# The order of the VectorE and ScalarE queues of a hybrid decoder trunk taken from the framework's timeline simulation

## The chip, the cores and the metric

The kernel runs on one core of a Trainium2 chip. The metric is the device time of one execution in microseconds (us). The kernel before took 970.87 us, the median of three runs (970.82 to 971.13).

A core has engines that work side by side, each through a queue of its own, strictly in order: TensorE (PE: matrix products; its weight loads are listed apart as PEld), VectorE (DVE: element-wise work, reductions), ScalarE (ACT: functions and scaled copies), GpSimd (POOL) and SyncE (SP), which here issues most DMAs. An instruction whose operands are not ready holds up everything behind it in the same queue, whether or not that could have started. This is what an order of a queue can cost, and it is the only thing that this change touches.

## The reference

Sixteen learned rows are set ahead of 512 tokens (L = 528 rows of 1024). Two layers follow, each a pre-normed branch that is added to its input, and a final norm; the sixteen rows are dropped.

```python
h = concat([meta, x])                                  # 528 x 1024
# layer 1: gated linear attention, 4 heads of 256 (k) x 512 (v)
q, k, v, z, g_lr = split(rmsnorm(h, g_norm[0]) @ gla_w_in)
lg = log_sigmoid(g_lr @ w_gate_up + b_gate) / 16       # decay, low rank
o  = chunked_scan(q, k, v, lg)                         # state S decayed per chunk
h  = h + (silu(z) * head_rms(o) * gla_gnorm) @ gla_w_out
# layer 2: differential softmax attention, 8 heads, two softmaxes each
q, k, v, z = split(rmsnorm(h, g_norm[1]) @ diff_w_in)
lam = exp(sum(lv[0]*lv[1])) - exp(sum(lv[2]*lv[3])) + lambda_init
a  = softmax(q0 k0 + bias) - lam * softmax(q1 k1 + bias)
h  = h + (silu(z) * head_rms(a @ v) * diff_gnorm * (1 - lambda_init)) @ diff_w_out
out = rmsnorm(h[16:], g_final)
```

## The kernel before

Everything is float32. A matrix product is made of rounded parts: `split` (L270 to L280) writes the high part of a tile with a ScalarE copy (L276) and the rest with a VectorE subtraction (L277), and TensorE adds high times high, high times low and low times high. So every weight block and every operand passes through ScalarE first and VectorE second before TensorE can use it. In the profile these are `wh` and `wl` (a pair of weight blocks), `a11h`, `a12h`, `a22h` and their `l` halves (single blocks), and `x`, `y`, `aT` (operands). `split3` (L402 to L411) does the same for narrow tiles `am`, `vm` and `cm` (ScalarE on L407 and L408, VectorE on L410 or L412).

The large input projections run as units of seven products in place of eight (class `Unit`). A product (`product`, L428, matmuls on L431) fills a PSUM bank `bx`, `by` or `bv`; there are two `bx` banks and one each of the others. When the first product of a unit ends, ScalarE copies it out as `u` (`partial`, L452), and only then can the bank be filled again; VectorE adds later products to that copy (L477 to L481). Sums of weight blocks are VectorE additions (L366). The first projections go without this scheme (`plain_unit`, L878).

The program starts by loading tokens, norming and turning them, and splitting them in pairs of tiles `x` (L776 scales a tile `y`, L277 makes the low parts). TensorE then computes the narrow projection of the decay (L1001, `bx<-x,kd`) from these tiles while the first value projection (L878) fills its gaps. Beside this, three short operations on VectorE read tiny tensors whose loads SP issues one after the other on L666, L668 and L671: `gn_sb` is halved (L1071), `dgs` is made from `dg_sb` (L1105), and `lt` is the product of the lambda vectors `lv` (L1097). They are first wanted a long time later: `lt` by a matmul near 143 us, `gn_sb` near 95 us. L796, L800 and L801 are differences and sums of halves of `y` for the units.

In layer 2 a head's work on one block of rows is: scores (matmuls on L400), VectorE adds the bias and finds the minimum (L1692), ScalarE takes the exponential (L1694), VectorE combines the two softmaxes (`st` on L1697 and L1698, the probabilities `p` on L1699), TensorE transposes `p` (L1707 and L1708) and multiplies by the values. The output projection of the head before runs between these (L400 with `bx`, `by`, `bv` as targets), and VectorE adds it to `keep` (L1783).

What sets the order. TensorE's order is written out by hand: `manual_schedule` for PE covers all of `trunk`, and a `Weaver` puts pieces of the projections between pieces of attention by estimated times. For VectorE and ScalarE the order is fixed by hand only at the start (L720 to L1031, for the instructions issued between these lines) and, on VectorE, for the last rows. Everywhere else the framework orders these two queues, and SP's, from dependencies, priorities and its estimate of when things are ready. The kernel steers it with priorities (`urgent`, `soon`, `at_once`, L254 to L265) and a few forced successions (`issue_after`). An instruction whose inputs the framework takes to be ready, and which appears much later in the program, can thus be moved ahead, as the three short operations are.

```python
    def urgent(fn, offset=100):

        def run(*a, **kw):
            with tc.high_priority(offset=offset):
                return fn(*a, **kw)
        return run
...
        @at_once
        def partial(self):
            t = T(up[0], [P, HT], F32, "u", bufs=3)[:, :self.n]
            W.moved = act.activation(t, self.bx[:, :self.n], AF.Copy, scale=self.sc)
            return t
```

Of the kernel before, what the change touches and what calls it, by code (L numbers as in the profile page):

```python
# [1944 lines left out]
def build(shapes):  # L1945
    import concourse.bacc as bacc

    nc = bacc.Bacc("TRN2", target_bir_lowering=False, num_devices=1, dynamic_dma_scratch_size=512)
    args = [nc.dram_tensor(f"in_{n}_dram", shp, F32, kind="ExternalInput").ap() for n, shp in shapes]
    args.append(nc.dram_tensor("out_0_dram", (1, NR, D), F32, kind="ExternalOutput").ap())  # L1950
    with tile.TileContext(nc) as tc:
        trunk(tc, *args)
    return nc

# [14 lines left out]
```

## Time and profile before

| what | value |
|---|---|
| median of 3 runs | 970.87 us |
| the profiled execution itself | 970.65 us |
| its span, first to last instruction | 968.9 us |
| outside the span | 1.75 us |
| TensorE busy | 957.2 us (99%) |
| VectorE busy | 778.6 us (80%) |
| ScalarE busy | 626.8 us (65%) |
| GpSimd busy | 44.9 us (5%) |
| mean granted TensorE clock | 0.999 |

A row of the timeline gives start, duration, engine, line, operation, output and inputs, a count where like neighbours are joined, and in brackets how long the engine idled before it and what ended that. A row of the windows gives a stretch, then for each engine its busy time and the number of its instructions, then the granted TensorE clock (1.00 is full), the share of the DMA engines and GB/s. A row of the waits gives who waited for whom: total, times, longest.

### The profile page before, as it was taken

How to read it: one execution, taken by the hardware profiler on the slowest of the kernel's cores; microseconds unless marked ns; L12 is line 12 of the kernel's file. 1: busy time of each engine (PE TensorE's matmuls, PEld its weight loads, DVE VectorE, ACT ScalarE, POOL GpSimd, SP SyncE). 2: the span in 40 equal slices, each digit the busy share in tenths (PEclk: the TensorE clock that was granted, in tenths of full speed). 3: DMA queues.
4: the chain of work that ended last, by engine and by line, in shares of the span. 5: the costliest groups of instructions: out<-in, count | busy, mean ns of one | idle time of the engine just before them, and what ended most of it. 6: DMA issues, size and time to landing. Idle time of an engine off the chain costs nothing.

```text
span 968.9 us, 18048 instructions
## 1 busy us (share of the span) xinstructions
PE 957.2 (99%) x6993; PEld 906.9 (94%) x6993; DVE 778.6 (80%) x1586; ACT 626.8 (65%) x1304; POOL 44.9 (5%) x68
## 2 busy tenths in 40 slices
PE   9999999999999999999999999999999999999997
PEld 8999999999999999998899998998999989989996
DVE  7989885886888787668997987968869769687785
ACT  7776755577647567656757776575675756755583
POOL 1000000000000000000001001000000000000001
PEclk9999999999999999999999999999999999999999
DMA  7322223635363236124355525243342341722212
GB/s 197 88 85 59 82 79 122 147 103 128 116 162 91 85 117 158 53 101 152 99 130 138 143 73 133 75 139 98 99 138 88 118 119 44 182 70 84 89 64 87
DMA packets 128522, 104.94 MB, mean 108 GB/s; under 512 B 51102, under 2 KB 112830, under 8 KB 128433
## 3 DMA queue, kind: packets, MB, share of 16 engines
q1 hardware_dynamic: 123104, 93.80, 35.1%
q10 hardware_dynamic: 5328, 9.95, 2.8%
q8 instruction: 56, 0.92, 0.4%
q14 instruction: 34, 0.27, 0.1%
HBM read 83.64 MB, written 11.80 MB: 99 GB/s over the span
## 4 chain that ended last, share of the span: by engine, by line
PE 88%; ACT 1%; DVE 1%; issue 1%; POOLq 0%; DVEq 0%
PE bx L431 19%; PE bv L431 12%; PE by L431 10%; PE bx L421 10%; PE ps L400 9%; PE bx L972 5%; PE bx L400 3%; PE bv L972 2%; PE by L972 2%; PE ps L1214 2%; PE by L400 2%; PE bv L400 2%; PE ps L1807 1%; PE bx L1807 1%; PE bv L421 1%; PE by L421 1%
## 5 line engine op out<-in xcount | busy, mean ns | idle before, releaser
L277 DVE TENSOR_TENSOR wl<-raw,wh 128x1024 fp32r<-128x1024 f32 x98 | 119.4, 1221 | 23.0 <-ACT wh L276 18.9
L276 ACT ACTIVATE wh<-raw 128x1024 fp32r<-128x1024 f32 x98 | 103.1, 1054 | 48.3 <-PE by L972 22.9
L431 PE MATMUL bv<-x,wh 128*128 128x264 f32 (+1 forms) x656 | 98.6, 287 | 0.0
L431 PE MATMUL bx<-x,wh 128*128 128x264 f32 (+1 forms) x640 | 95.6, 286 | 0.0
L431 PEld LDWEIGHTS bv<-x,wh 128*128 128x128 f32 x656 | 86.8, 189 | 0.6 <-DVE z L479 0.2
L431 PEld LDWEIGHTS bx<-x,wh 128*128 128x128 f32 x640 | 84.6, 188 | 0.7 <-ACT u L452 0.2
L452 ACT ACTIVATE u<-bx 128x264 f32<-128x264 f32 (+1 forms) x120 | 45.3, 379 | 35.5 <-PE bx L431 33.1
L1694 ACT ACTIVATE p<-p,st 128x528 f32<-128x528 f32 (+3 forms) x64 | 36.5, 570 | 41.7 <-DVE st L1692 41.4
L421 PE MATMUL bx<-x,wh 128*128 128x512 f32 (+1 forms) x256 | 62.4, 385 | 0.0
L277 DVE TENSOR_TENSOR wl<-sum,wh 128x1024 fp32r<-128x1024 f32 x41 | 50.1, 1221 | 10.6 <-ACT wh L276 10.5
L431 PE MATMUL bx<-x,wl 128*128 128x264 f32 (+1 forms) x320 | 54.1, 284 | 0.0
L431 PE MATMUL bv<-x,wl 128*128 128x264 f32 (+1 forms) x328 | 53.8, 284 | 0.1
L421 PEld LDWEIGHTS bx<-x,wh 128*128 128x128 f32 x256 | 44.4, 188 | 7.8
L276 ACT ACTIVATE wh<-sum 128x1024 fp32r<-128x1024 f32 x41 | 43.1, 1051 | 9.7 <-PE by L972 3.9
L431 PE MATMUL by<-x,a12h 128*128 128x264 f32 (+1 forms) x320 | 47.5, 286 | 0.1
L1730 POOL TENSOR_TENSOR st<-st,mhalf 128x1 f32<-128x1 f32 x32 | 25.5, 795 | 468.6 <-ACT on L1728 418.2
L431 PE MATMUL bx<-x,a11h 128*128 128x264 f32 (+1 forms) x320 | 46.6, 284 | 0.0
L431 PEld LDWEIGHTS bv<-x,wl 128*128 128x128 f32 x328 | 45.4, 188 | 0.3 <-issue 0.3
L431 PEld LDWEIGHTS bx<-x,wl 128*128 128x128 f32 x320 | 45.3, 188 | 0.3
L431 PEld LDWEIGHTS bx<-x,a11h 128*128 128x128 f32 x320 | 42.4, 188 | 0.6
L431 PEld LDWEIGHTS by<-x,a12h 128*128 128x128 f32 x320 | 42.1, 188 | 0.3 <-ACT t L1658 0.3
L276 ACT ACTIVATE a11h<-raw 128x512 fp32r<-128x512 f32 x41 | 25.7, 626 | 20.7 <-DMA raw<-in_diff_w_in_dram 7.9
(493 smaller groups left out, 2631.9 us busy)
## 6 DMA issues: line engine op xcount, KB each, us to landing
raw<-in_gla_w_in_dram SPq DMA_DIRECT2D x48, 512.0 KB, 4.5
raw<-in_diff_w_in_dram SPq DMA_DIRECT2D x42, 512.0 KB, 4.9
raw<-in_diff_w_in_dram SPq DMA_DIRECT2D x11, 1024.0 KB, 5.9
raw<-in_gla_w_out_dram SPq DMA_DIRECT2D x8, 1024.0 KB, 5.8
raw<-in_diff_w_out_dram SPq DMA_DIRECT2D x8, 1024.0 KB, 6.0
vd<-planes ACTq DMA_DIRECT2D x12, 268.0 KB, 5.8
vd<-keep ACTq DMA_DIRECT2D x12, 264.0 KB, 2.3
T<-bdr SPq DMA_DIRECT2D x8, 264.0 KB, 4.7
```

Source lines behind the costliest of these rows:

```text
L276: act.activation(hi, src, AF.Copy)
L277: dve.tensor_tensor(lo, src, hi.bitcast(F32), op=ALU.subtract)
L400: pe.matmul(ps, l, r, start=first and n == 0, stop=last and n == 2, **kw)
L421: pe.matmul(bank, a[:, k, :], b[k] if n0 is None else b[k][:, n0 + i * nn:n0 + (i + 1) * nn], start=n == 0 and ks[0] == 0, stop=n == len(t ...
L431: pe.matmul(bank[:, :x[q].shape[2]], w[p][:, k * P:(k + 1) * P], x[q][:, k, :], start=first and i == 0, stop=i == len(PASSES) - 1, skip_gr ...
L452: W.moved = act.activation(t, self.bx[:, :self.n], AF.Copy, scale=self.sc)
L972: pe.matmul(banks[i][:, :HT], h.t[p][:, k, mm * P:(mm + 1) * P], s.y[q][k][:, i * HT:(i + 1) * HT], start=n == 0, stop=n == len(PASSES) - 1)
L1214: pe.matmul(o, s.kd[:, i, kc], s.qs[:, i, t0:t0 + n], start=i == 0, stop=i == 1)
L1694: act.activation(p[:, :nk], p[:, :nk], AF.Exp, scale=-1.0, bias=st[:, m:m + 1], accum_out=st[:, 2 + m:3 + m])
L1730: pool.tensor_tensor(ms, ms, mhalf[:, :1], op=ALU.pow)
L1807: pe.matmul(ps[i], yp[hd][p][:, k, b * P:(b + 1) * P], wt[q][cs.start // 512][:, 2 * hd + k, cs.start % 512:(cs.stop - 1) % 512 + 1], star ...
```

## The change

One argument is added where `build` opens the framework's context. With it, the framework orders the queues that are not ordered by hand by a simulated timeline of the program in place of its plain estimate of readiness.

```diff
-    with tile.TileContext(nc) as tc:
+    with tile.TileContext(nc, schedule_with_timeline_sim=True) as tc:
         trunk(tc, *args)
```

No instruction is added or taken away, and none changes its shape. TensorE's and GpSimd's queues stay as they were. VectorE's and ScalarE's are reordered over the whole program (1810 and 1172 lines of difference), and on SP some DMAs change places with a neighbour (43 lines). Three places follow; a minus marks where a row stood, a plus where it stands now.

VectorE at the start of the program (about 17 to 25 us), where the tiles `x` are split in pairs:

```order
 L776 TENSOR_SCALAR y_42_291<-ps_276,g_sb 128x512
+L1071 TENSOR_SCALAR gn_sb<-gn_sb 128x16
+L1105 TENSOR_SCALAR dgs<-dg_sb 128x2
+L1097 TENSOR_TENSOR lt_4700<-lv 128x2
 L277 TENSOR_TENSOR x_1_77<-y_35_258,x_1_77 128x528
 L277 TENSOR_TENSOR x_34_257<-y_35_258,x_34_257 128x528
 L274 TENSOR_TENSOR wl_269<-raw_131,wh_268 128x1024
 L776 TENSOR_SCALAR y_42_291<-ps_286,g_sb 128x512
+L796 TENSOR_TENSOR y_35_258<-y_35_258 128x4x264
 L277 TENSOR_TENSOR x_2_78<-y_42_291,x_2_78 128x528
 L277 TENSOR_TENSOR x_3_79<-y_42_291,x_3_79 128x528
```

The three operations on the tiny loads moved up by some twenty rows to a place ahead of the second `x` pair, and L796 moved ahead of the third and fourth.

ScalarE at about 189 to 192 us, in a unit of layer 1; `u_5261` is the copy that frees a `bx` bank, `v` and `vm` are operands of the value products, `a11h` a weight block of the next unit:

```order
 L276 ACTIVATE wh_5225<-raw_4940 128x1024
-L575 ACTIVATE v_885_4661<-keep_83,tick_5242 128x4x128
+L575 ACTIVATE v_885_4661<-keep_83,tick_5242 128x4x128 x2
+L407 ACTIVATE vm_884_4660<-lands_5085,short 32x256
+L276 ACTIVATE a11h_5253<-raw_5081 128x512
+L408 ACTIVATE vm_884_4660<-lands_5085,short 32x256
 L452 ACTIVATE u_5261<-bx_5238 128x264
-L276 ACTIVATE a11h_5253<-raw_5081 128x512
-L575 ACTIVATE v_885_4661<-keep_83,tick_5242 128x4x128
 L276 ACTIVATE a12h_5315<-raw_5081 128x512
-L407 ACTIVATE vm_884_4660<-lands_5085,short 32x256
-L408 ACTIVATE vm_884_4660<-lands_5085,short 32x256
```

The copy `u_5261` now stands behind four instructions that stood behind it.

VectorE at about 862 to 870 us, in a head of layer 2; `p_13569` are the probabilities that TensorE transposes next. Before:

```order
L277 TENSOR_TENSOR wl_13605<-raw_13530,wh_13604 128x1024
L1699 SCALAR_TENSOR_TENSOR p_13569<-p_13581,st_13568,p_13569 128x528
L1692 ISA p_13626,st_13625<-ps_13627,T_13186 128x400
L1692 ISA st_13625 128x1
L1692 ISA p_13633,st_13625<-ps_13634,T_13186 128x400
L1692 ISA st_13625 128x1
L1783 TENSOR_TENSOR keep_8187<-keep_8187,by_13521 128x512
L1783 TENSOR_TENSOR keep_8187<-keep_8187,bv_13522 128x512
L1697 RECIPROCAL st_13625<-st_13625 128x1
L1783 TENSOR_TENSOR keep_8187<-keep_8187,bx_13523 128x512
L1698 SCALAR_TENSOR_TENSOR st_13625<-st_13625,lam 128x1
L277 TENSOR_TENSOR wl_13673<-raw_13530,wh_13672 128x1024
```

On the same engine at the same place of the program, after the change:

```order
L277 TENSOR_TENSOR wl_13605<-raw_13530,wh_13604 128x1024
L1697 RECIPROCAL st_13568<-st_13568 128x1
L366 TENSOR_TENSOR raw_13540<-raw_13540,sum_13682 128x4x128
L1783 TENSOR_TENSOR keep_8187<-keep_8187,by_13521 128x512
L1692 ISA p_13626,st_13625<-ps_13627,T_13186 128x400
L1692 ISA st_13625 128x1
L1783 TENSOR_TENSOR keep_8187<-keep_8187,bv_13522 128x512
L1698 SCALAR_TENSOR_TENSOR st_13568<-st_13568,lam 128x1
L1783 TENSOR_TENSOR keep_8187<-keep_8187,bx_13523 128x512
L277 TENSOR_TENSOR wl_13673<-raw_13530,wh_13672 128x1024
L1699 SCALAR_TENSOR_TENSOR p_13569<-p_13581,st_13568,p_13569 128x528
```

`p_13569` (L1699) moved from directly behind `wl_13605` to behind `wl_13673`, with the addition of `bx_13523` (L1783) between.

## The prediction

> **What bounds the kernel now.** I began with the page: busy times, the chain that ended last, and the two groups that speak of the parts made by ScalarE and VectorE.
>
> ```profile
> PE 957.2 (99%) x6993; PEld 906.9 (94%) x6993; DVE 778.6 (80%) x1586; ACT 626.8 (65%) x1304; POOL 44.9 (5%) x68
> ...
> PE 88%; ACT 1%; DVE 1%; issue 1%; POOLq 0%; DVEq 0%
> ...
> L277 DVE TENSOR_TENSOR wl<-raw,wh 128x1024 fp32r<-128x1024 f32 x98 | 119.4, 1221 | 23.0 <-ACT wh L276 18.9
> ...
> L452 ACT ACTIVATE u<-bx 128x264 f32<-128x264 f32 (+1 forms) x120 | 45.3, 379 | 35.5 <-PE bx L431 33.1
> ```
>
> TensorE is busy for 957.2 of 968.9 us, so it idles for 11.7 in all. The windows say where.
>
> ```profile
> 0.00:20.00 20.00, 18.08 (x130) 16.87 (x130) 14.31 (x35) 15.17 (x28) 3.42 (x11) 1.00 0.88 238
> 20.00:60.00 40.00, 39.66 (x329) 39.00 (x327) 35.69 (x54) 32.50 (x66) 0.00 (x0) 1.00 0.33 80
> ...
> 960.00:969.00 9.00, 2.12 (x16) 1.78 (x14) 3.58 (x8) 2.35 (x7) 0.86 (x1) 0.84 0.31 117
> ```
>
> The first row has 1.9 us of idle TensorE, the last 6.9, where nothing is left to multiply; everything between has 11.7 - 1.9 - 6.9 = 2.9. The waits of TensorE name most of it:
>
> ```profile
> PE bx L421 <- DVE wl L277: 0.7, 1, 0.7
> PE ps L1244 <- DVE vm L412: 0.7, 1, 0.7
> PE ps L1214 <- DVE kd L1218: 0.5, 1, 0.5
> ```
>
> So a new order of VectorE and ScalarE can give back some 2.9 us at most in the middle, while TensorE's order, which is written by hand, stands still and waits for whatever comes late. In 20 to 60 us VectorE is busy for 35.69 of 40: there it has little room to catch up. The question is thus where an operand comes later than TensorE's use of it, and each place is worked out as: how much later the row ends, less the slack that it had.
>
> **The start: three operations on tiny loads.** The order has L1071, L1105 and L1097 ahead of the second `x` pair, and L796 ahead of the third and fourth. Where they ran before, on VectorE:
>
> ```profile
> 18.33 1.33 DVE L277 TENSOR_TENSOR x<-y,x 128x528 fp32r<-128x528 f32 x2 [0.56 <-ACT x L276]
> ...
> 21.37 1.31 DVE L277 TENSOR_TENSOR x<-y,x 128x528 fp32r<-128x528 f32 x2
> ...
> 24.98 1.25 DVE L796 TENSOR_TENSOR y<-y 128x1056 f32<-128x1056 f32 x1
> ...
> 30.04 0.17 DVE L1071 TENSOR_SCALAR gn_sb<-gn_sb 128x16 f32<-128x16 f32 x1
> 30.12 0.16 DVE L1105 TENSOR_SCALAR dgs<-dg_sb 128x2 f32<-128x2 f32 x1
> ...
> 30.77 0.16 DVE L1097 TENSOR_TENSOR lt<-lv 128x2 f32<-128x2 f32 x1
> ```
>
> They take half a microsecond, but they need loads, and the last of these was issued by SP after the second pair had ended. The other row is of a like load, with its time from issue to landing at the end:
>
> ```profile
> 20.98 0.47 SPq L671 DMA_DIRECT2D lv<-in_diff_lam_dram  x1
> ```
>
> ```profile
> short<-in_short_dram SPq DMA_DIRECT2D x1, 2.2 KB, 1.8
> ```
>
> ```profile
> 22.50:23.00 0.50, 0.50 (x6) 0.50 (x5) 0.50 (x2) 0.50 (x2) 0.00 (x0) 1.00 0.48 20
> 23.00:23.50 0.50, 0.50 (x7) 0.50 (x6) 0.50 (x1) 0.50 (x2) 0.00 (x0) 1.00 0.04 0
> ```
>
> Its packets still run until 23.0 (DMA share 0.48, then 0.04), so `lv` lands at 23.0 at the earliest. By the like load it would be 20.98 + 0.47 + 1.8 = 23.25. `lv` is gathered element by element, and landing is told after the last packet, so I take 24.0 with 23.0 and 24.5 as ends. SP's issues up to `lv` keep their order, so this time stays. VectorE therefore halts from about 18 to 24.0, and with 0.16 for `lt` the pair of 18.33 starts at 24.2, 5.9 late. The pair of 21.37 is late by that and by L796's 1.25: 7.1. TensorE uses them here:
>
> ```profile
> 20.67 0.36 PE L1001 MATMUL bx<-x,kd 128*112 128x264 f32 x1
> ...
> 23.73 0.73 PE L1001 MATMUL bx<-x,kd 128*112 128x264 f32 x4
> ```
>
> The first half of the first pair ended at 19.0 and would end at 24.9: TensorE stands still at 20.67 for some 4.2. The second pair ended at 22.68; of the four matmuls at 23.73 the third and fourth, near 24.06, are the first to read it, so the slack was 1.4 and TensorE ends up 7.1 - 1.4 = 5.7 late. I take 5.5 (4.5 with the early landing, 6.2 with the late one). The projections of L878 that could fill the hole stand behind in TensorE's own queue.
>
> **The probabilities at 866 us.** L1699 of one block moved behind `wl_13673`, which waits for ScalarE.
>
> ```profile
> 863.80 0.76 DVE L1699 SCALAR_TENSOR_TENSOR p<-p,st,p 128x528 f32<-128x528 f32 x1
> ...
> 867.88 1.23 DVE L277 TENSOR_TENSOR wl<-raw,wh 128x1024 fp32r<-128x1024 f32 x1 [0.28 <-ACT wh L276]
> ```
>
> ```profile
> 866.58 0.60 PE L1707 MATMUL ps<-ident,p 128*128 128x128 f32 x4
> ```
>
> `wl` ends at 869.1 and L1699 then at 869.1 + 0.7 = 869.8; the transposes at 866.58 wait until then: 3.2. The same move with other blocks finds its time covered.
>
> **Copies `u` that free a bank.** At nine places L452 moved behind work that another product could wait for. The place that the order shows, on ScalarE and then TensorE:
>
> ```profile
> 189.52 0.37 ACT L452 ACTIVATE u<-bx 128x264 f32<-128x264 f32 x1
> 189.79 0.62 ACT L276 ACTIVATE a11h<-raw 128x512 fp32r<-128x512 f32 x1
> 190.31 0.71 ACT L575 ACTIVATE v<-keep,tick 128x512 fp32r<-128x512 f32 x1
> ...
> 191.45 0.49 ACT L407 ACTIVATE vm<-lands,short 32x256 fp32r<-32x256 f32 x1
> 191.97 0.51 ACT L408 ACTIVATE vm<-lands,short 32x256 fp32r<-32x256 f32 x1
> ```
>
> ```profile
> 190.61 1.14 PE L431 MATMUL bx<-x,wh 128*128 128x264 f32 x8
> ```
>
> `u` ended at 189.89, 0.72 ahead of the product that refills its bank. Four instructions go ahead of it, 0.5 apart for three of them and 0.6 for L575 (starts overlap a little): about 1.9 to 2.2. That leaves 1.2 to 1.5; I take 1.2. The same exchange comes once more a head later. In layer 2 the same unit meets the same exchange in four heads; the first:
>
> ```profile
> 643.96 0.37 ACT L452 ACTIVATE u<-bx 128x264 f32<-128x264 f32 x1
> ...
> 644.47 0.39 ACT L276 ACTIVATE aT<-ps 128x256 fp32r<-128x256 f32 x1
> 644.75 0.25 ACT L407 ACTIVATE am<-ps 32x128 fp32r<-32x128 f32 x1
> 645.01 0.27 ACT L408 ACTIVATE am<-ps 32x128 fp32r<-32x128 f32 x1
> ```
>
> ```profile
> 644.54 0.53 PE L431 MATMUL bx<-x,wh 128*128 128x264 f32 x3
> ```
>
> Here the slack is 644.54 - 644.33 = 0.21, and the three rows of `aT` and `am`, and the issue of a DMA, now go first: 0.8 for the three, 1.1 with the issue, so 0.6 to 0.9, and I take 0.8. The three other places of this kind lie between, and I give them 0.9. Sum: 2 x 1.2 + 4 x 0.8 + 3 x 0.9 = 8.3.
>
> **Five more places** have an operand of TensorE behind one to three instructions that now go first: L1255 twice and L1731 behind high parts of weights, L1403 behind a `wl` (1.22 by its group), the low part of `v` (L277) behind L801 early on. Not worked out each, they get the mean of the nine, 8.3 / 9 = 0.92: 4.6 (an estimate; nothing to 1.5 each).
>
> **What goes away, and what costs nothing.** Where TensorE waited for `wl`, `vm` and `kd`, the new order has these rows further ahead: at most 0.7 + 0.7 + 0.5 and some tenths, 2.2. On SP, the load of the bias table goes ahead of weights that are split only many rows later; at a wrong moment that would be one issue, about a microsecond. All other moves on VectorE and ScalarE stay inside the time by which their results lie ahead of TensorE; were that cover gone, each would cost what its neighbour lasts, 0.4 to 1.2.
>
> **The sum.** 5.5 + 3.2 + 8.3 + 4.6 - 2.2 = 19.4. Against the profiled execution, 970.65 + 19.4 = 990.05; the median of the runs is 0.22 above that execution, so 990.3.
>
> **The clock.** The granted clock could make it more. In the last window of the first table TensorE's final 2.12 us of work are over at 962.1, and then:
>
> ```profile
> 965.00:966.00 1.00, 0.00 (x0) 0.00 (x0) 0.10 (x1) 0.07 (x1) 0.00 (x0) 1.00 0.04 14
> 966.00:967.00 1.00, 0.00 (x0) 0.00 (x0) 0.00 (x0) 0.00 (x0) 0.00 (x0) 0.56 1.00 383
> ```
>
> With 0.56 as the mean of that microsecond the clock fell to half at 966.1, after 4.0 us of idle TensorE; the stall of the start would be 4.2. What half a clock costs is seen at the start, where the same eight transposes took 1.70 and later 1.09:
>
> ```profile
> 5.66 1.70 PE L705 MATMUL ps<-ident,qs 128*128 128x128 f32 x8
> ```
>
> ```profile
> 9.01 1.09 PE L705 MATMUL ps<-ident,ks 128*128 128x128 f32 x8 [0.19 <-ACT hT L711]
> ```
>
> The slow pace there lasted from the first matmul, near 1 us, to about 7, so a fall could cost half of 6 us, 3.0, or less where the clock comes back sooner: nothing to 3, and if it falls I take 2.5. Every other stall that I count is shorter than the 4.0 us of idleness that the trace shows ahead of the fall, so this can happen once. [...]
>
> **The rivals.**
> 1. Only the long halts count. Many of the fourteen places under 1.5 us have their price from one trace, and a queue that is late at one place has been early at the one before; if ScalarE's and VectorE's idle time (968.9 - 626.8 = 342 and 968.9 - 778.6 = 190 us) takes them up, 5.5 + 3.2 - 2.2 = 6.5 is left: 977.4. For it: `u` in its group idled 33.1 us behind TensorE, so ScalarE is mostly there early. Against it: the slack in the rows, 0.21 and 0.72, has that in it already. Chance 0.15.
> 2. The clock falls in the first stall: 990.3 + 2.5 = 992.8. For it: 4.2 of stall against 4.0 of idleness ahead of the fall that the trace shows. Against it: the margin is a few tenths, and an early landing of `lv` (23.0) shortens the stall to 3.2. Chance 0.15.
> 3. The other side: VectorE reaches L1071 no earlier than its loads have landed, because what stands ahead of the pair at 18.33 comes late as well, or `lv` lands sooner than its packets let me think, and ScalarE's moves fall into idle time. Then only the waits go: 970.87 - 2.2 = 968.7. It decides at a landing of `lv` by about 19, against an issue at 20.98. Chance 0.05.
> 4. The moves cancel, a few tenths each way, within 0.2% (1.9 us, about what a measurement of this kernel can tell from no change): 970.9. It needs the halt at the start to be absent too. Chance 0.03.
> 5. More late places than I followed, or longer ones, since 1810 and 1172 lines move: ten more at 0.92 give 999.5. Chance 0.10.
>
> My forecast, all places about as priced, has the rest, 0.52. The third rival alone is faster, 0.05; the fourth the same, 0.03; all others slower, 0.92. The bounds of the forecast: the start 4.5 to 6.2, the nine copies 0.6 to 1.5 each, the five 0 to 1.5, put it between 982 and 999. The range has to take in the first rival below and half of the fifth above: 976 to 1000.
>
> **What would show it.** Right: in the new trace VectorE idles some 5 us ahead of L1071 or L1097 near 18 to 24 us, TensorE waits about 4 for `x` on L1001 in one piece, and 3 for `p` on L1707 near 866 plus what came before; the waits list `u` on L452 with a total of several us; TensorE's idle time is near 31 instead of 11.7, its busy time within 1 us of 957.2. If busy time grows and the granted clock drops behind the first stall, it is the second rival. Wrong: no wait of TensorE above 1 us behind the first 10 us, or no idle VectorE at the start, or a total of `u` waits below 2.

## The result and the profile after

The kernel after the change takes 999.29 us (median of four runs, 998.64 to 1001.76), the kernel before 970.85: a ratio of 1.030, with an interval of 1.028 to 1.032. The forecast was 990.3 with a range of 976 to 1000. The direction and the mechanism were right; 28.4 us were lost where 19.4 were forecast.

The profiled execution took 998.96 us (span 997.2). The engines' busy times on its page:

```profile
PE 964.9 (97%) x6993; PEld 909.5 (91%) x6993; DVE 778.8 (78%) x1586; ACT 631.1 (63%) x1304; POOL 41.9 (4%) x68
```

VectorE's and ScalarE's busy times are within 5 us of before. TensorE's idle time went from 11.7 to 997.2 - 964.9 = 32.3 us, and its busy time rose by 7.7. Part of that is time that the clock was at half, as the windows below show. The rest lies in how a row is drawn: a matmul's row is longer than the distance to the next matmul, so that at a wait of TensorE about 0.15 us of the delay is counted as busy (near 864 us before, a matmul of 0.39 us is followed by the next after 0.24). Behind the first 15 us there are 31 waits at which TensorE falls behind its times of before by 0.2 us or more; at these it falls behind by 27.4 us in all, while its idle time grows by 22.6.

TensorE's own waits, as total, times and longest; before the change none of them was above 1.2, and that one (L631, at the very start) is still there:

```profile
PE bx L431 <- ACT u L452: 6.9, 9, 1.4
PE bx L1001 <- DVE x L277: 3.4, 3, 2.5
PE ps L1707 <- DVE p L1699: 3.4, 2, 3.2
PE ps L1308 <- ACT t L1255: 2.7, 3, 1.2
PE ps L1044 <- DVE v L277: 1.3, 1, 1.3
...
PE ps L1214 <- DVE kd L1218: 1.0, 2, 0.8
PE ps L400 <- DVE st L1692: 0.9, 1, 0.9
...
PE ps L1737 <- ACT on L1731: 0.8, 1, 0.8
```

All but two of these lines are places of the forecast: `u`, the `x` pairs, `p`, and four of its five smaller ones (the fifth, L1403, waits 0.3). The waits for `kd` and `st` are not. At the start, VectorE's queue:

```profile
17.93 0.74 DVE L776 TENSOR_SCALAR y<-ps,g_sb 128x512 f32<-128x512 f32 x1
22.51 0.17 DVE L1071 TENSOR_SCALAR gn_sb<-gn_sb 128x16 f32<-128x16 f32 x1 [3.84 <-DMA gn_sb<-in_gla_gnorm_dram]
22.85 0.17 DVE L1105 TENSOR_SCALAR dgs<-dg_sb 128x2 f32<-128x2 f32 x1 [0.17 <-DMA dg_sb<-in_diff_gnorm_dram]
23.49 0.16 DVE L1097 TENSOR_TENSOR lt<-lv 128x2 f32<-128x2 f32 x1 [0.47 <-DMA lv<-in_diff_lam_dram]
23.57 1.32 DVE L277 TENSOR_TENSOR x<-y,x 128x528 fp32r<-128x528 f32 x2
```

and TensorE behind it:

```profile
24.32 0.38 PE L1001 MATMUL bx<-x,kd 128*112 128x264 f32 x1 [2.53 <-DVE x L277]
...
28.52 0.38 PE L1001 MATMUL bx<-x,kd 128*112 128x264 f32 x1 [0.58 <-DVE x L277]
29.14 0.38 PE L1001 MATMUL bx<-x,kd 128*112 128x264 f32 x1 [0.24 <-DVE x L277]
```

Three operations of 0.17 us held the queue from 18.6 to 23.6 because each stood in wait for a tiny load. The pair of 18.33 us now starts at 23.57. Near 200 us (190 before) `u` is last of five on ScalarE, and TensorE's refill of its bank waits for it:

```profile
200.01 0.51 ACT L408 ACTIVATE vm<-lands,short 32x256 fp32r<-32x256 f32 x1
200.54 0.39 ACT L452 ACTIVATE u<-bx 128x264 f32<-128x264 f32 x1
```

```profile
200.98 1.25 PE L431 MATMUL bx<-x,wh 128*128 128x264 f32 x8 [1.32 <-ACT u L452]
```

The place that was at 866 us, and the windows right behind it:

```profile
892.15 0.66 PE L1707 MATMUL ps<-ident,p 128*128 128x128 f32 x4 [3.18 <-DVE p L1699]
```

```profile
892.00:893.00 1.00, 0.85 (x7) 0.79 (x8) 0.68 (x3) 0.19 (x1) 0.00 (x0) 0.99 0.39 90
893.00:894.00 1.00, 1.00 (x4) 0.81 (x3) 0.38 (x2) 1.00 (x4) 0.00 (x0) 0.50 0.77 213
...
896.00:897.00 1.00, 1.00 (x5) 0.82 (x4) 0.00 (x0) 0.00 (x0) 0.00 (x0) 0.81 0.28 90
```

The granted clock (the third number from the end) is 0.50 from 892.97 to 896.39: a half clock for 3.4 us behind this stall. Behind the start's stall it stayed at 1.00 in this execution (20 to 30 us).

TensorE executes the same rows in the same order before and after, so each row's start after less its start before is how late TensorE is there, and where that difference steps up lies a place that costs. For instance, the row of L1001 that starts at 24.32 started at 20.67 before: 24.32 - 20.67 = 3.65, of which 0.9 was there already in the first 15 us, so the step is 2.7 to 2.8. The steps, put together:

| where | forecast | measured steps |
|---|---|---|
| the start (L1001: 2.7 + 0.8 + 0.5) | 5.5 | 4.0 |
| `p` at 866 us | 3.2 | 3.4 |
| `u`, ten places where the forecast counted nine (0.3, 1.2, 1.5, 0.5, 1.4, 1.3, 0.7, 0.8, 0.8, 0.7) | 8.3 | 9.2 |
| `v` 1.5, L1255 1.2 and 1.4, L1731 1.0, L1403 0.6 | 4.6 | 5.7 |
| waits that went (0.6, 0.7, 0.9, 0.2) | -2.2 | -2.4 |
| the first 15 us 1.0 (a late load and a half clock), the half clock behind 866 us 1.6 | a rival, 2.5 | 2.6 |
| places not followed: `hT` near 175 us 1.4, `kd` at 357 0.95, `st` at 939 0.95, and smaller ones (difference) | a rival | 5.8 |
| **sum** | **19.4** | **28.3** |

The sum is the lateness of TensorE's last rows, and 970.65 + 28.3 = 998.95 is the profiled execution's own time. The 1.0 of the first 15 us belongs to this execution and not to the order: in the profiles of a_p, a_u and half1 (below), which have the same order there, TensorE is within 0.1 us of before at 15 us.

### The profile page after: what moved, and what is told of

It reads as the page before. It is cut to its first block, busy times and chain, and to the rows that moved or that the text cites. A ratio compares the mean times of both kernels' runs of the same rounds, so it can differ in the third digit from the quotient of the medians.

```text
span 997.2 us, 18081 instructions
## 1 busy us (share of the span) xinstructions
PE 964.9 (97%) x6993; PEld 909.5 (91%) x6993; DVE 778.8 (78%) x1586; ACT 631.1 (63%) x1304; POOL 41.9 (4%) x68
## 5 line engine op out<-in xcount | busy, mean ns | idle before, releaser
L277 DVE TENSOR_TENSOR wl<-raw,wh 128x1024 fp32r<-128x1024 f32 x98 | 119.5, 1220 | 22.9 <-ACT wh L276 11.7
L1730 POOL TENSOR_TENSOR st<-st,mhalf 128x1 f32<-128x1 f32 x32 | 22.9, 716 | 483.5 <-ACT on L1728 403.4
L366 DVE TENSOR_TENSOR sum<-raw 128x512 f32<-128x512 f32 x41 | 28.1, 686 | 16.4 <-DMA raw<-in_gla_w_in_dram 10.6
```

The source lines that it names most:

```text
L277: dve.tensor_tensor(lo, src, hi.bitcast(F32), op=ALU.subtract)
L366: dve.tensor_tensor(o, a, b, op=ALU.add)
L1730: pool.tensor_tensor(ms, ms, mhalf[:, :1], op=ALU.pow)
```

## The experiments

The theory is that of the prediction: the loss is a sum of separate places, each of which costs what its operand comes late to TensorE. The rival is a loss of the order as a whole: VectorE and ScalarE fall behind over long stretches, so that single places neither cost nor give back their step.

To take one place at a time, VectorE's and ScalarE's queues are written out as lists of the program's instructions, and each instruction is queued behind the one before it in its list. The lists cost next to nothing by themselves: with the order of before up to 860 us, TensorE in b_p is there within 0.3 us of its time before. The two queues were cut into stretches that hold the same instructions before and after; 155 of VectorE's and 141 of ScalarE's differ in their order. The new order on one engine alone was not tried.

```diff
+        for n in (f"I-{n}" for n in queue):
...
+            if b in last:
+                tc.add_manual_dep(found[n], last[b], mybir.DependencyInfo(
+                    mybir.DependencyClass.NoSync, mybir.DependencyReason.DATA), reason="in_order")
+            last[b] = n
```

### The start

**b_tiny**, against before, on VectorE:

```diff
 L776 TENSOR_SCALAR y_42_291<-ps_276,g_sb 128x512
+L1071 TENSOR_SCALAR gn_sb<-gn_sb 128x16
+L1105 TENSOR_SCALAR dgs<-dg_sb 128x2
+L1097 TENSOR_TENSOR lt_4700<-lv 128x2
 L277 TENSOR_TENSOR x_1_77<-y_35_258,x_1_77 128x528
...
 L1026 TENSOR_TENSOR a_20_157<-bx_314,a_56_422 16x264
-L1071 TENSOR_SCALAR gn_sb<-gn_sb 128x16
-L1105 TENSOR_SCALAR dgs<-dg_sb 128x2
 L1026 TENSOR_TENSOR a_20_157<-bx_315,a_56_422 16x264
-L1097 TENSOR_TENSOR lt_4700<-lv 128x2
```

> The order of before on VectorE and ScalarE, with one move: the three operations on tiny loads (L1071, L1105, L1097) stand ahead of the second x pair, as after the change; L796 stays. First theory (the loss is a sum of places, each of which costs what its operand comes late): VectorE halts until lv lands near 23.5 us, TensorE waits some 2.5 to 3 us for x on L1001, and the time is 970.85 + 2.7 = 973.5. Second theory (the loss comes from queues that fall behind over long stretches; one halt is made up for by the idle time of VectorE behind it): below 971.9.

Measured: 975.18 us, 4.3 more than before (ratio 1.0047, 1.0031 to 1.0064). TensorE's rows:

```profile
24.25 0.38 PE L1001 MATMUL bx<-x,kd 128*112 128x264 f32 x1 [3.38 <-DVE x L277]
24.46 0.60 PE L705 MATMUL ps<-ident,v 128*128 128x128 f32 x4
24.86 0.38 PE L1001 MATMUL bx<-x,kd 128*112 128x264 f32 x1
25.08 0.37 PE L878 MATMUL bv<-x,wh 128*128 128x264 f32 x1
25.25 0.42 PE L878 MATMUL by<-x,wh 128*128 128x264 f32 x1
```

The wait is 3.4, larger than the first theory's 2.5 to 3; and from 25 us a matmul of L878 takes 0.42 where it took 0.28 before. After the change, matmuls of L717 take 0.42 at a granted 0.50 (at 9.07 and 9.28 us) where before they took 0.27 at 1.00; the mean clock of b_tiny's execution is 0.997, in executions of before 0.998 to 0.999. The lower clock is the second part of the 4.3. Nothing is made up for later: three operations of a sixth of a microsecond, moved by themselves, cost over 4 us. The second theory is out here.

**a_start**, against after: VectorE's whole stretch of 18 to 31 us as before.

```diff
-L1071 TENSOR_SCALAR gn_sb<-gn_sb 128x16
-L1105 TENSOR_SCALAR dgs<-dg_sb 128x2
-L1097 TENSOR_TENSOR lt_4700<-lv 128x2
 L277 TENSOR_TENSOR x_1_77<-y_35_258,x_1_77 128x528
...
-L796 TENSOR_TENSOR y_35_258<-y_35_258 128x4x264
 L277 TENSOR_TENSOR x_2_78<-y_42_291,x_2_78 128x528
```

> The order after the change, with the first disordered stretch of VectorE (the three operations on tiny loads and L796, 18 to 31 us) put back as before. First theory: the steps of 2.7, 0.8 and 0.5 us at 20 to 24 us go, nothing else moves: 999.3 - 4.0 = 995.3. Second theory: what is won at the start is lost again later, less than 1.5 us stay: above 997.8.

Measured: 995.54 us (993.74 to 996.46), 3.75 less than after. By the first theory it would be 4.0; the four executions lie 2.7 us apart, so the agreement is no closer than that.

### The probabilities at 866 us

**b_p** is before with this stretch as after (the rows of the third place in the section on the change, and the neighbouring rows of ScalarE); **a_p** is after with it as before.

```diff
-L1699 SCALAR_TENSOR_TENSOR p_13569<-p_13581,st_13568,p_13569 128x528
...
 L1783 TENSOR_TENSOR keep_8187<-keep_8187,bx_13523 128x512
 L277 TENSOR_TENSOR wl_13673<-raw_13530,wh_13672 128x1024
+L1699 SCALAR_TENSOR_TENSOR p_13569<-p_13581,st_13568,p_13569 128x528
```

> The order of before, with the one stretch around 866 us (probabilities of L1699 behind wl and keep on VectorE, and the neighbouring rows of ScalarE) as after the change. First theory: TensorE waits 3.2 to 3.5 us for p on L1707: 970.85 + 3.4 = 974.3, and 975.9 where the clock falls to half behind the stall for one window (1.6 us more). Second theory: with TensorE not late from earlier places, the stall is under 1.5: below 972.4.

> The order after the change, with the stretch around 866 us put back as before. First theory: the stall of 3.4 us and the half clock behind it (1.6 us) both go: 999.3 - 5.0 = 994.3. If the half clock had another reason, it stays and the time is 995.9. Second theory: less than 1.5 us go: above 997.8.

Measured: b_p 975.86 us (975.57 to 975.91), 5.0 more than before; a_p 993.91 (992.87 to 994.77), 5.4 less than after. Both are the first theory's number with the half clock in it, and b_p carries the argument, since its four executions lie within 0.4 us. In a_p they lie 1.9 us apart, and its profile (mean clock 0.995) has another half clock, of 6.8 us, behind the start's stall of 3.3. In b_p the stall and the clock behind it:

```profile
870.11 0.66 PE L1707 MATMUL ps<-ident,p 128*128 128x128 f32 x4 [3.15 <-DVE p L1699]
```

```profile
871.00:872.00 1.00, 1.00 (x4) 0.81 (x3) 0.41 (x3) 1.00 (x4) 0.00 (x0) 0.50 0.89 230
872.00:873.00 1.00, 1.00 (x4) 0.81 (x3) 1.00 (x2) 0.39 (x2) 0.00 (x0) 0.50 0.95 290
```

**b_p_fill** and **b_p_fill12** ask whether idle TensorE is what lowers the clock: b_p with 24 and with 12 empty products in the stall.

```diff
             pt, pm = ps_tile(), ps_tile()
+            if uid[0] == 2469:
+                for _ in range(12):
+                    FILLERS.append(int(pe.matmul(pt[:, :P], ones, ones, start=True, stop=True).ins.name[2:]))
             for j in range(b + 1):
```

> The kernel with the one stretch around 866 us as after the change, and 24 empty products (ones times ones into the bank that the transposes fill anyway) on TensorE ahead of the transposes that wait for p. They take about 2.7 us and lie in a stall of 3.3, so they move nothing. If the half clock behind the stall comes from idle TensorE, it does not come, and the time is that of before plus 3.3: 974.2, 1.6 below the kernel without them (975.86). If it has another reason: 975.9.

Measured: 977.71 us. This is outside both numbers of the expectation: the products took 5.52 us where 2.7 were reckoned, since each is issued as two (48 rows of L1708), and overran the stall. The clock stayed at 1.00 from 866 to 875 us, but what that saves can't be read from a time that has the overrun in it. b_p_fill12 has half as many products.

> The kernel with the one stretch around 866 us as after the change, and 12 empty products ahead of the transposes that wait for p. By the run with 24, which took 5.52 us and so overran the stall by 2.1, 12 take 2.8 and lie inside it. If the half clock comes from idle TensorE, it does not come and nothing is overrun: 970.9 + 3.3 = 974.2, against 975.86 without the products. If the half clock has another reason: 975.9. If products of this kind delay the other engines: above 976.

Measured: 973.99 us (973.88 to 974.95), 1.9 below b_p, and 0.2 from the forecast for a clock that stays full. Against the kernel before, measured beside each of the two, the loss is 2.8 us in place of 5.0. TensorE's rows and the window to set beside that of b_p:

```profile
866.58 2.84 PE L1708 MATMUL ps<-ones 128*128 128x128 f32 x24
869.89 0.66 PE L1710 MATMUL ps<-ident,p 128*128 128x128 f32 x4 [0.47 <-DVE p L1699]
```

```profile
871.00:872.00 1.00, 1.00 (x6) 0.84 (x5) 0.62 (x3) 0.99 (x5) 0.00 (x0) 1.00 0.90 234
```

The transposes start as late as in b_p (869.89 against 870.11); only the idleness is gone, and with it the half clock. This shows what the half clock costs behind one stall: some 2 us by the times (1.9 against b_p, 2.2 when each is set against its own before), 1.6 by the steps of the trace.

### The copies that free a bank

**a_u** is after with ten copies `u` put back; at 191 us, for instance:

```diff
 L276 ACTIVATE wh_5225<-raw_4940 128x1024
-L575 ACTIVATE v_885_4661<-keep_83,tick_5242 128x4x128 x2
+L575 ACTIVATE v_885_4661<-keep_83,tick_5242 128x4x128
+L452 ACTIVATE u_5261<-bx_5238 128x264
+L575 ACTIVATE v_885_4661<-keep_83,tick_5242 128x4x128
 L407 ACTIVATE vm_884_4660<-lands_5085,short 32x256
 L276 ACTIVATE a11h_5253<-raw_5081 128x512
 L408 ACTIVATE vm_884_4660<-lands_5085,short 32x256
-L452 ACTIVATE u_5261<-bx_5238 128x264
```

> The order after the change, with ten copies u (L452) put back to their old neighbours on ScalarE: two at 95 and 108 us, the two of 191 and 291, those of 255 and 552, and the four of layer 2 (645, 707, 771, 834). First theory (the places add): the steps that the trace after the change has at them, 0.3 + 1.2 + 1.5 + 0.5 + 1.4 + 1.3 + 0.7 + 0.8 + 0.8 + 0.7 = 9.2 us, go: 999.3 - 9.2 = 990.1. Second theory (the rows that went ahead of u are needed as much, so that TensorE waits for them instead): less than 5 go, above 994.3.

Measured: 994.12 us, but from 991.20 to 998.07; the second theory's bound was 994.3. By the median this run settles nothing. Its four executions have mean clocks of 0.997, 0.995, 0.991 and 0.992, from the shortest to the longest: the longer two spent more of their time at half clock. The trace (of an execution with 0.997) has no wait for `u` left, and a second wait for `p`:

```profile
PE ps L1707 <- DVE p L1699: 5.2, 2, 3.2
```

```profile
576.23 0.66 PE L1707 MATMUL ps<-ident,p 128*128 128x128 f32 x4 [1.96 <-DVE p L1699]
```

After the change the same transposes (561 us before) waited 0.17 for `p`, because TensorE came late from the `u` ahead of them. With that `u` on time TensorE is there before `p`, and 1.8 of the 9.2 are lost again. Another 0.9 goes at 118 us, where TensorE now waits for `t` of L1255, and 0.9 at 615, where the wait for `on` of L1731 grows from 0.8 to 1.7 (a_start, which leaves the copies as after, has that longer wait too). Set against the trace after the change, TensorE is 0.8 us later at 60 us and 5.5 earlier at 860: 6.3 of the 9.2 are gained. So a part of the second theory holds: some of the places that the change made late hide behind others.

This execution also has the wait at 866 us, of 3.19, and the clock did not fall behind it:

```profile
886.67 0.66 PE L1707 MATMUL ps<-ident,p 128*128 128x128 f32 x4 [3.19 <-DVE p L1699]
```

```profile
888.00:889.00 1.00, 1.00 (x6) 0.82 (x5) 0.84 (x3) 0.95 (x4) 0.00 (x0) 1.00 0.96 271
```

**b_u** asks the same from the other side: before with six of the stretches as after (the two of 191 and 291 us and the four of layer 2).

```diff
 L589 ACTIVATE planes_10920<-t_10815 128x1072
-L452 ACTIVATE u_10974<-bx_10874 128x264
-L590 DMA vd_10921<-planes_10920 128x1072 x2
 L276 ACTIVATE aT_1954_10958<-ps_10952 128x256
 L407 ACTIVATE am_10957<-ps_10953 32x128
 L408 ACTIVATE am_10957<-ps_10953 32x128
+L590 DMA vd_10921<-planes_10920 128x1072
+L452 ACTIVATE u_10974<-bx_10874 128x264
```

> The order of before, with the six stretches of ScalarE around the copies u of 191, 291, 645, 707, 771 and 834 us as after the change. First theory (each place costs what its operand comes late, and no stall is long enough for the clock to fall): the steps of the trace after the change, 1.5 + 1.4 + 0.7 + 0.8 + 0.8 + 0.7 = 5.9 us: 970.8 + 5.9 = 976.7, within 1 us. Second theory (the copies cost only where the other queues are late too): below 973.8.

Measured: 977.00 us (976.85 to 977.21), 6.0 more than before (ratio 1.0061, 1.0046 to 1.0077). Its waits:

```profile
PE bx L431 <- ACT u L452: 4.7, 6, 1.4
```

Six places, six waits, and the clock does not fall behind any of them (mean clock 0.998, in executions of before 0.998 to 0.999). For these six, the price of the copies stands as forecast.

### The sum of the places

**half1** is after up to the end of layer 1 and before from there: the lists of both engines are spliced at 449 us, where they hold the same instructions.

```diff
-ORDER = layer 1 as after, layer 2 as after
+ORDER = layer 1 as after, layer 2 as before
```

> The order after the change up to the end of layer 1 (449 us of the trace of before), the order of before from there on. First theory: the lateness of TensorE at that place of the trace after the change, 16.3 us less some 1 us that the clock lost in the first 15 us, and nothing behind it: 970.85 + 15.3 = 986.2, up to 2 us more where the clock falls behind a stall. Second theory (queues that fall behind and never catch up): layer 2, though in the old order, starts late on VectorE and ScalarE and loses more: above 990.

Measured: 986.83 us (986.18 to 989.17), 0.6 from the first theory. In its trace TensorE is 15.0 us later than before at 449 us and 15.5 at the end: layer 2 loses next to nothing by the lateness of layer 1.

**a_back** is after with 86 stretches around the late places as before; 210 of the 296 that differ stay as after the change.

```diff
-ORDER = 296 stretches as after
+ORDER = 210 stretches as after, 86 as before
```

> The order after the change, with the 86 disordered stretches around the places where TensorE came late (42 of 155 on VectorE, 44 of 141 on ScalarE) put back as before; the other 210 stay as after the change. First theory: all that was lost is in those places, and the waits that the change removed near 389, 470 and 498 us stay removed: 970.85 - 1.8 = 969.1, below before. Second theory (a wide loss of the order as a whole): above 973.

Measured: 970.59 us (969.69 to 974.82), a ratio to before of 0.9997 (0.9988 to 1.0006). The whole loss of 28.4 lies in those 86 stretches. It came out 1.5 above the first theory. New places, made by mixing the orders, are the likely reason: the profiled execution, the longest of the twelve, has four waits of 0.8 to 1.1 us that neither order has, but how many of them the other executions have is not shown. Two of the four follow each other closely near the end, and the clock falls behind them (mean clock 0.996, in the other eleven 0.997 to 0.999):

```profile
939.24 0.56 PE L400 MATMUL ps<-k,q 128*128 128x144 f32 x3 [1.07 <-DVE aT L277]
940.74 0.56 PE L400 MATMUL ps<-k,q 128*128 128x144 f32 x3 [0.94 <-DVE am L410]
```

### What the new order gains

**gains** is before with two stretches of VectorE as after:

```diff
+L412 SCALAR_TENSOR_TENSOR vm_1307_7225<-lands_7602,short,vm_1307_7225 32x256
 L479 TENSOR_TENSOR t_7725<-bv_7695,u_7693 128x264
-L412 SCALAR_TENSOR_TENSOR vm_1307_7225<-lands_7602,short,vm_1307_7225 32x256
...
+L277 TENSOR_TENSOR wl_8591<-raw_8342,wh_8590 128x1024
 L277 TENSOR_TENSOR x_1513_8555<-hT_90,x_1512_8554 128x4x256
...
-L277 TENSOR_TENSOR wl_8591<-raw_8342,wh_8590 128x1024
```

> The order of before, with two stretches of VectorE as after the change: 459 to 469 us (a low part wl of L277 ahead of the x parts behind L1464) and 388 us (vm of L412 ahead of an addition). First theory: the two waits of 0.9 and 0.7 us that TensorE had there go and nothing else moves: 970.85 - 1.6 = 969.3. Second theory: the time shows up again at the next operand: above 970.4.

Measured: 969.63 us, a ratio of 0.9987 (0.9978 to 0.9996). Of TensorE's two waits one went, that for `wl` at 470 us (a step of 0.9); the other stayed:

```profile
PE ps L1244 <- ACT vm L408: 0.5, 1, 0.5
```

Before the change it was put down to VectorE's `vm` (L412). With that row earlier it is ScalarE's half of the same tile (L408) that comes last: both have to move.

**best** takes both, and with them the neighbouring stretches of VectorE and ScalarE at 376 to 392 us, ScalarE's at 459 to 469, VectorE's at 80 to 87, and two rows of L1218:

```diff
 L452 ACTIVATE u_7613<-bx_7483 128x264
+L575 ACTIVATE v_1308_7226<-keep_83,tick_7626 128x4x128 x2
+L407 ACTIVATE vm_1307_7225<-lands_7455,short 32x256
+L408 ACTIVATE vm_1307_7225<-lands_7455,short 32x256
 L452 ACTIVATE u_7631<-bx_7616 128x264
-L575 ACTIVATE v_1308_7226<-keep_83,tick_7626 128x4x128 x2
...
+L276 ACTIVATE wh_7794<-raw_7786 128x1024
 L934 ACTIVATE t_7758<-t_7726 128x528
-L276 ACTIVATE wh_7794<-raw_7786 128x1024
```

> The order of before, with the stretches as after the change that showed a gain of TensorE and no loss: VectorE and ScalarE at 80 to 87, 376 to 392 and 459 to 469 us, and the first two rows of L1218 near 352 us ahead of a low part of a weight block. First theory: the gains add, 0.3 + 0.5 + 0.7 + 0.8 = 2.3 us: 970.8 - 2.3 = 968.5. Second theory: only the largest of them stays: above 969.8.

Measured: 968.76 us (968.41 to 969.30) beside 971.00 of before on the same chip: a ratio of 0.9976 (0.9967 to 0.9985). It is faster than the kernel before by 2.2 us, about what the prediction gave as the most that the middle of the program can give back (2.9). What is left of TensorE's waits behind the first 15 us is small:

```profile
PE ps L1214 <- DVE kd L1218: 0.4, 1, 0.4
PE bx L878 <- DVE a L1026: 0.3, 1, 0.3
```

## Why the prediction was right, and where it was short

**The bound.** TensorE's order stands still, so a new order elsewhere can only take its waits away or add to them. This held: at most 2.4 us went, and the rest that was measured is waits of TensorE, the clock behind them, and the 1.0 of the first 15 us.

**The signs.** VectorE idles 4.5 us in all ahead of L1071, L1105 and L1097, `p` waits 3.18, `u` 6.9 in all, and TensorE's idle time is 32.3, all near what was said. Two signs failed: TensorE waits 2.5 for `x` in one piece and 3.4 in all where about 4 in one piece was said, and its busy time rose by 7.7 where "within 1 us" was said, for the two reasons given under the result.

**The sum.** The places that were priced came to 19.9 against 19.4, closer than the working deserves: the start was priced 1.5 too high, and the copies and the smaller places 2.0 too low. The 8.4 us that are missing are two things that stood among the rivals, the clock and the places not followed, and the measured time lies 0.7 us inside the upper end of the range.

**The start, 5.5 against 4.0.** The steps are the ones named; the term was mis-sized. The forecast let `lv` land at 24.0; it landed by 23.49, with the last packets between 23.3 and 23.4, and the first 15 us had made both engines about 1.0 late already, which takes as much off the halt. In b_tiny, which is on time at 15 us, the wait is 3.4. The wait is not the same in every execution: in half1 it is 3.1, in a_u 4.2.

**866 us, 3.2 against 3.4**, and alone 3.15 in the wait of b_p: right, place and size.

**The copies, 8.3 against 9.2**, and 6.0 alone for six of them, for which the forecast had 2 x 1.2 + 4 x 0.8 = 5.6: right. What was too simple is that the forecast took each place to be independent; a_u shows that with the copies on time other operands come late in their place, and 6.3 of the 9.2 are gained.

**The five smaller ones, 4.6 against 5.7**, were priced by the mean of the others and came out a little dearer, `v` at 37 us most (1.5).

**The waits that go, 2.2 against 2.4**: right.

**The step that failed is the one on the clock**: "Every other stall that I count is shorter than the 4.0 us of idleness that the trace shows ahead of the fall, so this can happen once". It took the only fall that the trace showed for a threshold. In the profiled execution after the change the clock fell behind the stall of 866 us (a wait of 3.18) and not behind the start's 2.53; in b_tiny it fell behind 3.38, in b_p behind 3.15. At 866 us that adds 1.6 to 2.2 us, and b_p_fill12, where the filled stall leaves the clock at 1.00, shows the cause. So the second rival was right that a stall of this change lowers the clock, took 2.5 us for it, and had the place wrong for the profiled execution; that its 2.5 is near the 2.6 of the table is luck. The 2.5 was read from the slow pace at the start. The windows of before print a clock of 1.00 there, so that this pace was half a clock was the author's reading; at a granted 0.50 (after, 9.49 us) eight transposes of L705 took 1.91, against the 1.09 of before at 1.00. Behind the start's stall the clock did fall in the profiles of b_tiny, a_p, a_u and half1 (in half1 its mean is 0.96 from 20 to 60 us). By the traces waits of 3.15 and 3.18, shorter than those 4.0, were enough.

**The other part that was short** is the fifth rival: places not followed, 5.8 us in the trace, none above 1.4. They were given a chance of 0.10 and come on top of the forecast rather than in its place. They were not taken apart one by one; a_back shows only that, with all the late places, they lie in its 86 stretches. The first rival, that most places are hidden in idle time, is refuted by b_u for the six copies that it moves, and the third and fourth by the result.

## What to carry to other kernels

When one engine is busy 99% of the time in an order that is fixed, a new order for its helpers has little to win and much to lose, as this one from a simulated timeline had: list each operand that now stands behind something else, compare its end with its use, and sum. Look first for short operations on late loads that are pulled ahead in a strict queue, and for copies that free a bank. Having found where the new order helps and where it hurts, take it stretch by stretch: here a dozen of 296 made the kernel 0.24% faster, while the whole cost 3%. Price the places as a sum, but do not expect that mending one gives back its whole step: the next late operand may stand right behind it.

## What the runs showed of the hardware

A stall of TensorE of some 3 us can cost more than its length: behind waits of 3.15 (b_p) and 3.18 (after) the granted clock stood at 0.50 for 3.4 us, from 870.88 to 874.30 and from 892.97 to 896.39, and it fell behind the 3.38 of b_tiny as well. Behind the 3.19 of a_u it did not, so the length of the wait does not decide alone. In the 3.41 us ahead of the fall after the change, TensorE's busy time (the second number) was 0.82; it is 0.77 in b_p and 0.89 in b_tiny:

```profile
889.56:892.97 3.41, 0.82 (x6) 0.79 (x7) 3.12 (x6) 1.34 (x4) 0.00 (x0) 1.00 0.09 24
```

So whether the clock falls varies between executions of one kernel, and the time with it. The mean clock tells how much: after the change the execution of 998.64 us had 0.997 and that of 1001.76 had 0.993. A clock lower by 0.004 over 997 us is 4.0 us of work that was not done, of the size of the 3.1 us between them.

In the first 15 us of the execution after the change the clock fell as well, although TensorE was busy for 0.71, 0.78, 0.89 and 0.27 of the four microseconds before; the last of these and the first at half clock:

```profile
8.00:9.00 1.00, 0.27 (x2) 0.28 (x3) 0.93 (x4) 1.00 (x4) 0.15 (x1) 0.96 0.99 393
9.00:10.00 1.00, 1.00 (x7) 1.00 (x6) 0.33 (x3) 1.00 (x3) 0.56 (x1) 0.50 1.18 266
```

The half clock lasted 3.41 us, from 8.92 to 12.33, and in the 3.41 us ahead of it TensorE was busy for 2.05, far more than the 0.77 to 0.89 above. In a_back the clock fell behind waits of 1.07 and 0.94, which end at 939.24 and 940.74. So the busy time ahead of a fall, as the profile counts it, does not decide alone either, and what does is not settled by these runs.
